# Gate pieces, head matrices, z accumulators and final states of one mLSTM and S5 step, placed anew

## The chip, the core and the metric

The kernel runs on one core of one Trainium2 chip. The metric is the device time of one execution in microseconds. Five engines work beside one another, each through its own instructions in order: TensorE (PE, matrix products and transposes), VectorE (DVE), ScalarE (ACT), GpSimd (POOL) and SyncE (SP), whose queue here issues nearly all DMAs.

## The reference, cut to what matters

One step of a layer with two head groups that share the input `a = rmsnorm(h)`, for a prompt of 1024 tokens and 32 sample tokens (8 sequences of 4):

```python
proj = a @ w_in
x_m, z_m, o_m, i_pre, f_pre, x_s, z_s = jnp.split(proj, SPLIT_IDX, axis=-1)
...
logf = jax.nn.log_sigmoid(f_pre.astype(f32) + b_fgate.astype(f32))
hA, C1, n1, m1 = mlstm_chunkwise(q, k, v, i_t, logf, C0.astype(f32), n0.astype(f32), m0.astype(f32))
...
yB, sre1, sim1 = s5_scan(x_s.astype(f32), sre0, sim0, lam_re, lam_im, log_dt,
                         B_re, B_im, C_re, C_im, s5_D)
yB = jax.nn.gelu(yB)
yB = yB * jax.nn.sigmoid(yB @ w_glu.astype(f32) + b_glu.astype(f32))
yB = yB * jax.nn.silu(z_s.astype(f32))
h = h + jnp.concatenate([hA, yB], axis=-1).astype(h.dtype) @ w_out
...
h = h + jax.nn.sigmoid(h @ w_ple_gate) * e
```

`mlstm_chunkwise` needs for each token and head a running maximum and a running sum of the gates `i` and `f` (the "gate arithmetic" below). `s5_scan` runs 32 channel groups with a 64-dim complex state each. The final states of both groups are outputs.

## The kernel before

Activations lie transposed in SBUF, split into a high and a low fp32 part (`aTh`, `aTl`), and each product of fp32 matrices is three matmuls (`mm3`, L118 to L121: high by high, low by high, high by low). The weights are split likewise: ScalarE casts the high part (`hi_*`, L112), and DVE or POOL subtracts it for the low part (`lo_*`, L113). The tokens are cut into three chunks of 256, 384 and 416 columns (`CH`).

In order of time the program has these stages: the input tiles, their norms and the first o-gate tile, to about 62 us; the projection x_s and the tables of the S5 part, to about 100 us; the S5 part, to about 266 us; the mLSTM heads, which begin with the projection x_m (`ps_xm`), to about 470 us; the output projection and the last gate to the end.

The S5 part works on eight units u0 to u7 of four channel groups. A unit (`s5_run`) loads its inputs `us`, multiplies them by a table `WV` into the accumulators `vr`, `vi`, rotates on DVE (`w`, L616 to L623), scans, rotates back (`v`, `xs_`), and multiplies by `tz` and `cs` into `py`; ScalarE and DVE then form the GELU (`sq`, `y`). Between these steps PE gets filler: the rest of the o gate (`o_rest`), four tiles of z_s and two of z_m. `take(cols)` draws matmuls from the filler until that many columns are issued; `FILL_A`, `FILL_B`, `FILL_C` are the amounts behind the three steps of a unit. A tile of z has three accumulators (`ps_zs`, `ps_zm`; two buffers); each is emptied by a tanh on ScalarE (L702) and a product on DVE that reads the accumulator again (L703), and the result `ztmp` goes to HBM.

`s5_final` ends the part: it forms the sample's last states (`sfr`, `sfi`), transposes them on PE (`tpf`), copies them on ScalarE into `ob`, of tag "w2" with one buffer, and sends them out; the prompt's state `fin` follows (`tpg`). Then the rest of the filler is drawn.

The instructions are put in order by a scheduler that goes by priorities and a cost estimate. Within `tc.manual_schedule` PE keeps the written order, and only instructions that are recorded outside of it (there the gate arithmetic and the head matrices) may be placed between. The gate arithmetic (L785 to L893) is recorded behind the S5 part: transposes `tpr` to rows, running sums and maxima in `rw`, `bb_`, `g_`, `M_`, a reshaping through a DMA (`er` from `ends`, L820 on), `mc`, `mp`, then `nM`, `nML`; transposes `tpk`; and the same for the sample (`tps`, `sr`, `srw`, `d_srow`, `senm`, `tpq`, `scol`). `smb` (L1296) reads `d_srow` later. The head matrices (L894 to L915) are `Gm`, four products of w_q and w_k from transposes `tpw` copied to `wT` and products `gps`, and `scT`, the transposed conv state (`tpv`).

Of the kernel before, what the change touches and what calls it, by code (L numbers as in the profile page):

```python
# [24 lines left out]
FILL_A, FILL_B, FILL_C = 15000, 2400, 4000  # L25
# [4 lines left out]
def tile_hymba(ctx: ExitStack, tc: tile.TileContext, d: dict, o: list):  # L30
# [636 lines left out]
    def s5_final():  # L667
# [23 lines left out]
        dma(o_pim[0, 0], ob[:, 64:128])  # L691

# [15 lines left out]
    def filler():  # L710
# [58 lines left out]
    SC = 128.0 ** -0.5
    colv = mlc.tile([128, 3, 32], F32, name="colv")  # L770
    scol = mlc.tile([96, 2, 4], F32, name="scol")
    senm = mlc.tile([128, 1], F32, name="senm")
    d_row = dram.tile([2, 4, 8, 128], F32, name="d_row")
    d_srow = dram.tile([3, 4, 32], F32, name="d_srow")
    cmask = mlc.tile([128, 128], F32, name="cmask")


    def gt_(shape, name):
        return gp_.tile(shape, F32, name=name)

    G.memset(cmask, 0.0)
    G.affine_select(out=cmask, in_=cmask, pattern=[[1, 128]], compare_op=ALU.is_ge, fill=NEG, base=0,
                    channel_multiplier=-1)

    fx = gates[:, 4:8, :]  # L785
    na, uu, zz, ww, pp = (gt_([128, 4, 9], n) for n in ("na", "uu", "zz", "ww", "pp"))
    V.scalar_tensor_tensor(na, fx, -1.0, fx, op0=MUL, op1=MIN)
    A.activation(uu, na, AF.Exp)
    V.tensor_scalar(zz, uu, 2.0, None, op0=ADD)
    V.reciprocal(zz, zz)  # L790
    V.tensor_tensor(zz, zz, uu, op=MUL)
    V.tensor_tensor(ww, zz, zz, op=MUL)
    V.tensor_scalar(pp, ww, 1.0 / 13, None, op0=MUL)
    for c_ in (11, 9, 7, 5, 3):
        V.scalar_tensor_tensor(pp, pp, 1.0 / c_, ww, op0=ADD, op1=MUL)
    V.scalar_tensor_tensor(pp, pp, 1.0, zz, op0=ADD, op1=MUL)
    lf = gt_([128, 4, 9], "lf")
    V.tensor_scalar(lf, fx, 0.0, None, op0=MIN)
    V.scalar_tensor_tensor(lf, pp, -2.0, lf, op0=MUL, op1=ADD)
    gin = gt_([128, 2, 4, 8], "gin")  # L800
    V.tensor_copy(gin[:, 0], gates[:, 0:4, 0:8])
    V.tensor_copy(gin[:, 1], lf[:, :, 0:8])

    rw = gp_.tile([32, 2, 128], F32, tag="rw", name="rw", bufs=1)
    tp = pg([32, 2, 128], "tpr")
    for i in range(2):
        T.transpose(tp[:, i, :], gin[:, i].rearrange("p h c -> p (h c)"), ident)
    V.tensor_copy(rw, tp)
    one1 = gt_([32, 1], "one1")
    V.memset(one1, 1.0)  # L810
    one = one1.to_broadcast([32, 128])
    bb_, g_, M_, m_ = (gt_([32, 128], n) for n in ("bb_", "g_", "M_", "m_"))
    V.tensor_tensor_scan(bb_, one, rw[:, 1, :], 0.0, op0=MUL, op1=ADD)
    V.tensor_tensor(g_, rw[:, 0, :], bb_, op=SUB)
    V.tensor_tensor_scan(M_, one, g_, -3.0e38, op0=MUL, op1=MAX)
    ends = gt_([32, 2], "ends")
    V.tensor_copy(ends[:, 0:1], M_[:, 127:128])
    V.tensor_copy(ends[:, 1:2], bb_[:, 127:128])
    er4 = gt_([4, 8, 2], "er4")
    dma(er4, ends)  # L820
    mc = gt_([4, 9], "mc")
    V.memset(mc[:, 0:1], 0.0)
    V.tensor_tensor_scan(mc[:, 1:9], er4[:, :, 0], er4[:, :, 1], 0.0, op0=MAX, op1=ADD)
    with tc.high_priority():
        dma(o_pm[0, 0].unsqueeze(1), mc[:, 8:9])
    mp = gt_([32, 1], "mp")
    dma(mp, mc[:, 0:8])
    V.tensor_scalar(M_, M_, mp, None, op0=MAX)
    V.tensor_tensor(m_, M_, bb_, op=ADD)
    nM = gp_.tile([32, 2, 128], F32, tag="rw", name="nM", bufs=1)  # L830
    V.tensor_scalar(nM[:, 0, :], M_, -1.0, None, op0=MUL)
    A.activation(nM[:, 1, :], M_, AF.Exp, scale=-1.0, bias=mp)
    with tc.high_priority():
        dma(d_row.rearrange("x h c t -> (h c) x t"), nM)
    nML = gt_([32, 1], "nML")
    V.tensor_copy(nML, nM[:, 0, 127:128])
    wl_, en_ = gt_([32, 128], "wl_"), gt_([32, 128], "en_")
    A.activation(wl_, g_, AF.Exp, bias=nML)
    A.activation(en_, m_, AF.Exp, scale=-1.0)
    tp = pg([128, 3, 32], "tpk")  # L840
    for i, t_ in enumerate((g_, wl_, en_)):
        T.transpose(tp[:, i, :], t_, ident[:32, :32])
    V.tensor_copy(colv[:, 0:3], tp)

    gs = gt_([32, 2, 4], "gs")
    V.tensor_copy(gs[:, 0], gates[:32, 0:4, 8])
    V.tensor_copy(gs[:, 1], lf[:32, :, 8])
    sr = gt_([4, 2, 32], "sr")
    tp = pg([4, 2, 32], "tps")
    for i in range(2):  # L850
        T.transpose(tp[:, i, :], gs[:, i, :], ident[:32, :32])
    V.tensor_copy(sr, tp)
    rs1, rs2 = gt_([4, 8, 4], "rs1"), gt_([4, 8, 4], "rs2")
    V.memset(rs1, 1.0)
    V.memset(rs1[:, :, 0:1], 0.0)
    V.memset(rs2, 0.0)
    V.memset(rs2[:, :, 0:1], NEG)
    m0 = gt_([4, 8], "m0")
    dma(m0, d["state_mlstm_m"][0].rearrange("b h -> h b"))
    sb, sg, sM, sm_ = (gt_([4, 8, 4], n) for n in ("sb", "sg", "sM", "sm_"))  # L860

    def fl(ap):
        return ap.rearrange("p b t -> p (b t)")

    V.tensor_tensor_scan(fl(sb), fl(rs1), sr[:, 1, :], 0.0, op0=MUL, op1=ADD)
    V.tensor_tensor(fl(sg), sr[:, 0, :], fl(sb), op=SUB)
    V.tensor_tensor_scan(fl(sM), fl(rs2), fl(sg), NEG, op0=ADD, op1=MAX)
    m0b = m0.unsqueeze(2).to_broadcast([4, 8, 4])
    V.tensor_tensor(sM, sM, m0b, op=MAX)
    V.tensor_tensor(sm_, sM, sb, op=ADD)  # L870
    smo = gt_([4, 8], "smo")
    V.tensor_copy(smo, sm_[:, :, 3])
    with tc.high_priority():
        dma(o_sm[0].rearrange("b h -> h b"), smo)
    srw = gt_([4, 3, 32], "srw")
    sx1, sx2, swl = gt_([4, 8, 4], "sx1"), gt_([4, 8, 4], "sx2"), gt_([4, 8, 4], "swl")
    V.tensor_scalar(srw[:, 0, :], fl(sM), -1.0, None, op0=MUL)
    V.tensor_tensor(sx1, m0b, sM, op=SUB)
    A.activation(srw[:, 1, :], fl(sx1), AF.Exp)
    A.activation(srw[:, 2, :], fl(sm_), AF.Exp, scale=-1.0)  # L880
    with tc.high_priority():
        dma(d_srow.rearrange("x h t -> h x t"), srw)
    V.tensor_tensor(sx2, sg, sM[:, :, 3:4].to_broadcast([4, 8, 4]), op=SUB)
    A.activation(swl, sx2, AF.Exp)
    tp = pg([32, 2, 4], "tpq")
    T.transpose(tp[:, 0, :], fl(sg), ident[:4, :4])
    T.transpose(tp[:, 1, :], fl(swl), ident[:4, :4])
    for i in range(3):
        V.tensor_copy(scol[32 * i:32 * i + 32, 0, :], tp[:, 0, :])
        V.tensor_scalar(scol[32 * i:32 * i + 32, 1, :], tp[:, 1, :], SC, None, op0=MUL)  # L890
    dma(senm, d_srow[2].rearrange("h t -> (h t)").unsqueeze(1))
    wq = mlc.tile([128, 4, 128], F32, name="wq")
    wk = mlc.tile([128, 4, 128], F32, name="wk")  # L893
# [664 lines left out]
```

## Time and profile before

| | us |
|---|---|
| median of 3 runs | 691.0 |
| lowest, highest run | 689.8, 698.46 |
| the profiled execution | 693.87 |
| its span | 692.2 |
| PE busy | 623.8 |
| DVE busy | 435.8 |
| ACT busy | 264.1 |

The span runs from the first to the last instruction of the profiled execution; the execution's time is 1.67 us longer. The profiled execution took 2.87 us more than the median. Busy times are sums over the instructions of an engine; matmuls overlap, so the time in which PE is busy is shorter than the sum of its instructions. The mean clock granted to PE was 0.958 of full speed.

### The profile page before, as it was taken

The numbers are of one execution on the slowest core, as the hardware profiler recorded it, in microseconds if no ns is written. First come the engines' busy times: TensorE is split into PE (matmuls) and PEld (weight loads), VectorE is DVE, ScalarE is ACT, GpSimd is POOL, SyncE is SP. The second block draws the span as 40 slices with busy tenths as digits, with TensorE's granted clock in tenths as the row PEclk, the third lists the DMA queues.
The fourth block names the chain that finished last, engine by engine and source line by source line (L and its number), as shares of the span: only waits on it lengthen the run. The fifth ranks groups of instructions, "written<-read, shape, count | busy, mean of one in ns | idle before, by whom it ended". The sixth has DMA issues, their size and how long they took to land.

```text
span 692.2 us, 11563 instructions
## 1 busy us (share of the span) xinstructions
PE 623.8 (90%) x4068; PEld 547.7 (79%) x4068; DVE 435.8 (63%) x1289; ACT 264.1 (38%) x643; POOL 163.5 (24%) x173
## 2 busy tenths in 40 slices
PE   3999998987998949999996898769999999999995
PEld 2898898976988949998995687636888876778885
DVE  4789788979898640578667898754222323656435
ACT  5555633323332314534345545344111424433232
POOL 5813000000000115224323655544110204001000
PEclk9999999989999979999998899969999999999999
DMA  8804435452444338200546637457631237313121
GB/s 276 234 24 97 118 87 163 116 122 57 107 114 113 94 80 236 61 1 32 159 129 176 198 91 229 142 175 214 206 118 65 92 132 259 107 52 131 41 83 61
DMA packets 109679, 86.34 MB, mean 125 GB/s; under 512 B 33263, under 2 KB 92547, under 8 KB 109622
## 3 DMA queue, kind: packets, MB, share of 16 engines
q1 hardware_dynamic: 109622, 85.61, 41.3%
q8 instruction: 32, 0.52, 0.4%
q14 instruction: 25, 0.20, 0.1%
HBM read 60.10 MB, written 25.49 MB: 124 GB/s over the span
## 4 chain that ended last, share of the span: by engine, by line
PE 62%; DVE 16%; DMA 9%; issue 4%; SPq 4%; ACT 3%; POOL 1%; POOLq 0%; DVEq 0%; ACTq 0%
PE po L1379 4%; PE po L1378 4%; PE po L1377 4%; SPq L36 4%; PE po L1486 4%; PE po L1487 3%; PE po L1488 3%; PE ps_xm L120 2%; PE ps_xm L121 2%; PE ps_xm L119 2%; PE ps_zm L120 2%; PE ps_zm L119 2%; PE ps_zm L121 2%; PE ps_o L119 2%; PE ps_o L120 2%
## 5 line engine op out<-in xcount | busy, mean ns | idle before, releaser
L1486 PE MATMUL po<-wgh,hTh 128*128 128x512 f32 (+1 forms) x136 | 52.1, 383 | 0.7 <-ACT g_t L1489 0.7
L1488 PE MATMUL po<-wgh,hTl 128*128 128x512 f32 (+1 forms) x136 | 51.5, 379 | 0.0
L1487 PE MATMUL po<-wgl,hTh 128*128 128x512 f32 (+1 forms) x136 | 51.4, 378 | 0.0
L119 PE MATMUL ps_o<-hi_o,aTh 128*128 128x264 f32 (+2 forms) x136 | 41.2, 303 | 1.5 <-DVE gates L235 0.8
L120 PE MATMUL ps_o<-lo_o,aTh 128*128 128x264 f32 (+2 forms) x136 | 39.8, 293 | 1.4 <-POOL lo_o L113 1.4
L121 PE MATMUL ps_o<-hi_o,aTl 128*128 128x264 f32 (+2 forms) x136 | 39.7, 292 | 0.0
L119 PE MATMUL ps_zs<-aTh,hi_zs 128*128 128x256 f32 (+2 forms) x96 | 34.0, 354 | 4.8 <-DVE ztmp L703 4.7
L119 PE MATMUL ps_xs<-aTh,hi_xs 128*128 128x256 f32 (+2 forms) x96 | 31.9, 332 | 3.1 <-DVE gates L235 1.7
L1377 PE MATMUL po<-woh,mh 128*128 128x512 f32 x80 | 33.3, 416 | 1.0 <-ACT mh L1364 1.0
L119 PE MATMUL ps_zm<-aTh,hi_zm 128*128 128x256 f32 (+2 forms) x96 | 32.9, 343 | 0.1
L121 PE MATMUL ps_zm<-aTh,lo_zm 128*128 128x256 f32 (+2 forms) x96 | 32.4, 338 | 0.0
L120 PE MATMUL ps_zm<-aTl,hi_zm 128*128 128x256 f32 (+2 forms) x96 | 32.3, 337 | 0.0
L1378 PE MATMUL po<-wol,mh 128*128 128x512 f32 x80 | 32.3, 404 | 0.0
L121 PE MATMUL ps_zs<-aTh,lo_zs 128*128 128x256 f32 (+2 forms) x96 | 32.3, 337 | 0.0
L1379 PE MATMUL po<-woh,mlo 128*128 128x512 f32 x80 | 32.3, 403 | 0.0
L120 PE MATMUL ps_zs<-aTl,hi_zs 128*128 128x256 f32 (+2 forms) x96 | 32.3, 336 | 0.0
L119 PE MATMUL ps_xm<-aTh,hi_xm 128*128 128x256 f32 (+2 forms) x96 | 31.9, 332 | 0.0
L121 PE MATMUL ps_xm<-aTh,lo_xm 128*128 128x256 f32 (+2 forms) x96 | 31.8, 332 | 0.0
L120 PE MATMUL ps_xm<-aTl,hi_xm 128*128 128x256 f32 (+2 forms) x96 | 31.6, 329 | 0.0
L121 PE MATMUL ps_xs<-aTh,lo_xs 128*128 128x256 f32 (+2 forms) x96 | 31.3, 326 | 0.0
L120 PE MATMUL ps_xs<-aTl,hi_xs 128*128 128x256 f32 (+2 forms) x96 | 31.0, 322 | 0.0
L1486 PEld LDWEIGHTS po<-wgh,hTh 128*128 128x128 f32 x136 | 25.6, 188 | 6.0 <-ACT g_t L1489 1.0
(591 smaller groups left out, 1931.7 us busy)
## 6 DMA issues: line engine op xcount, KB each, us to landing
xt<-in_x_prompt SPq DMA_DIRECT2D x15, 512.0 KB
Wraw<-in_w_out SPq DMA_DIRECT2D x16, 256.0 KB
Wraw<-in_w_ple_gate SPq DMA_DIRECT2D x16, 256.0 KB
d_h<-xt SPq DMA_DIRECT2D x8, 512.0 KB
h_t<-d_h SPq DMA_DIRECT2D x8, 512.0 KB
out<-g_t SPq DMA_DIRECT2D x14, 256.0 KB
mt<-d_m SPq DMA_DIRECT2D x10, 256.0 KB
d_us<-xs SPq DMA_DIRECT2D x32, 72.0 KB
```

The lines of the kernel that those rows point to most:

```text
L36: nc.sync.dma_start(out, in_)
L119: T.matmul(ps, wh, xh, start=first, stop=False)
L120: T.matmul(ps, wh, xl, start=False, stop=False)
L121: T.matmul(ps, wl, xh, start=False, stop=last)
L1377: T.matmul(ps, mh[:, k % 4, :], hi, start=k == 4, stop=False)
L1378: T.matmul(ps, mh[:, k % 4, :], lo, start=False, stop=False)
L1379: T.matmul(ps, mlo[:, k % 4, :], hi, start=False, stop=k == 3)
L1486: T.matmul(ps[:, :b - a], hTh[i][:, k, :], hi[:, ws], start=k == 4, stop=False)
L1487: T.matmul(ps[:, :b - a], hTh[i][:, k, :], lo[:, ws], start=False, stop=False)
L1488: T.matmul(ps[:, :b - a], hTl[i][:, k, :], hi[:, ws], start=False, stop=k == 3)
```

## The change

It does five things. The gate arithmetic becomes a generator `gates_g` in four pieces, and one piece is recorded at the end of each of the units u0 to u3, inside the block with the written PE order. The head matrices and their loads are recorded ahead of the S5 part. In the filler's z tiles ScalarE copies the accumulator to a tile `zc` in SBUF (one buffer), and DVE reads that. `s5_final` becomes a generator with filler between its pieces, and its second `ob` uses the tag "zr". The filler amounts grow. The bodies of the gate arithmetic and of the head matrices are unchanged; lines behind the S5 part get numbers 17 higher.

```diff
--- before.py
+++ after.py
-FILL_A, FILL_B, FILL_C = 15000, 2400, 4000
+FILL_A, FILL_B, FILL_C = 15500, 3600, 4400
...
             V.tensor_tensor(t_, t_, f1, op=ADD)
-        for t_, dst in ((sfr, o_sre), (sfi, o_sim)):
+        yield
+        for t_, dst, tag in ((sfr, o_sre, "w2"), (sfi, o_sim, "zr")):
             tp = pt([128, 128], "tpf")
             T.transpose(tp, t_.rearrange("p b q -> p (b q)"), ident)
-            ob = s5.tile([128, 128], F32, tag="w2", name="ob", bufs=1)
+            ob = s5.tile([128, 128], F32, tag=tag, name="ob", bufs=1)
             A.copy(ob, tp)
             dma(dst[0].rearrange("b (q g) p -> (b q) (g p)", g=2), ob)
+            yield
         tp = pt([32, 128], "tpg")
         T.transpose(tp, fin, ident)
         ob = s5.tile([32, 128], F32, tag="w3", name="ob2")
         A.copy(ob, tp)
         dma(o_pre[0, 0], ob[:, 0:64])
         dma(o_pim[0, 0], ob[:, 64:128])
+        yield
...
-    def z_tile_g(c0, idx, name):
+    def z_tile_g(c0, idx, name, free=None):
...
             A.activation(tz_[:, :n], ps[:, :n], AF.Tanh, scale=0.5)
+            if free is not None:
+
+                zc = free.tile([128, 416], F32, tag="zc", name="zc", bufs=1)
+                A.copy(zc[:, :n], ps[:, :n])
+                ps = zc
             V.scalar_tensor_tensor(tz_[:, :n], tz_[:, :n], 1.0, ps[:, :n], op0=ADD, op1=MUL)
...
+    def gates_g():
+
+        G.memset(cmask, 0.0)
...
+        rw = gp_.tile([32, 2, 128], F32, tag="rw", name="rw", bufs=1)
+        yield
+        tp = pg([32, 2, 128], "tpr")
...
+        A.activation(en_, m_, AF.Exp, scale=-1.0)
+        yield
+        tp = pg([128, 3, 32], "tpk")
...
+        A.activation(swl, sx2, AF.Exp)
+        yield
+        tp = pg([32, 2, 4], "tpq")
...
+        dma(senm, d_srow[2].rearrange("h t -> (h t)").unsqueeze(1))
+        yield
...
-            yield from z_tile_g(2056 + 128 * j, 4 + j, f"zs{j}")
+            yield from z_tile_g(2056 + 128 * j, 4 + j, f"zs{j}", s5)
         for h in range(2):
-            yield from z_tile_g(512 + 128 * h, h, f"zm{h}")
+            yield from z_tile_g(512 + 128 * h, h, f"zm{h}", s5)
...
+    for h in range(4):
+        tp = pg([128, 2, 128], "tpw")
...
+        A.mul(Gm[:, h, :], gps, SC)
     lo_engine[0] = V
     with tc.manual_schedule(engines={mybir.EngineType.PE}):
+        gate = gates_g()
         ins = [s5_in(u) for u in range(8)]
...
             take(FILL_C)
-        s5_final()
-        for _ in fill:
-            pass
+            if u < 4:
+                next(gate)
+        end = s5_final()
+        for n in (5000, 3000, 3000, 1 << 30):
+            prod(end)
+            take(n)
```

On PE at the end of S5, before (`ps_zm` is filler, `tpf` and `tpg` the transposes of final states):

```order
L119 MATMUL ps_zm_3071<-aTh_105,hi_zm_3008 128x384
L120 MATMUL ps_zm_3071<-aTl_108,hi_zm_3008 128x384
L121 MATMUL ps_zm_3071<-aTh_105,lo_zm_3009 128x384
L682 MATMUL tpf<-ident,sfr 128x128
L682 MATMUL tpf<-ident,sfi 128x128
L687 MATMUL tpg<-ident,fin 32x128
L119 MATMUL ps_zm_3071<-aTh_105,hi_zm_3008 128x384
```

The same place after the change:

```order
L121 MATMUL ps_zm_3287<-aTh_106,lo_zm_3212 128x416
L683 MATMUL tpf<-ident,sfr 128x128
L119 MATMUL ps_xm<-aTh_104,hi_xm_3419 128x256
...
L120 MATMUL ps_xm<-aTl_108,hi_xm_3419 128x384
L683 MATMUL tpf<-ident,sfi 128x128
L121 MATMUL ps_xm<-aTh_105,lo_xm_3420 128x384
...
L120 MATMUL ps_xm<-aTl_109,hi_xm_3419 128x416
L689 MATMUL tpg<-ident,fin 32x128
L121 MATMUL ps_xm<-aTh_106,lo_xm_3420 128x416
```

The three transposes stood together ahead of the rest of the z filler; now the filler has ended before the first, and matmuls of the first x_m tile lie between them.

On PE ahead of the products `vr` of u3, after the change (`tpW` makes the table `WV`, `tpk` and `tps` belong to the gates):

```order
L557 MATMUL tpW<-ident,wt 128x128 x4
...
L793 MATMUL tpk<-ident,g__2001 128x32
L793 MATMUL tpk<-ident,wl__2026 128x32
L793 MATMUL tpk<-ident,en__2027 128x32
L802 MATMUL tps<-ident,gs 4x32 x2
L612 MATMUL vr<-us,WV 64x144 x4
```

Before, these transposes lay among the filler of u0 and u1, wherever the scheduler had put them; `tpr` now stands in the same way ahead of the `vr` of u2, and `tpq` ahead of that of u4.

On DVE in u2, after the change (`er` comes by DMA from `ends`):

```order
L764 TENSOR_TENSOR g__2001<-rw,bb__2000 32x128
L768 COPY ends<-bb__2000 32x1
...
L767 COPY ends<-M__2002 32x1
L640 TENSOR_TENSOR xs__2061<-v_2064,v_2065 64x2x128 x2
L596 TENSOR_TENSOR rti<-rBr,rAi 128x256
L596 TENSOR_TENSOR rtr<-rBr,rAr 128x256
L641 TENSOR_TENSOR xs__2061<-v_2066,v_2067 64x2x128 x2
L773 SCALAR_TENSOR_TENSOR mc<-er_2010 4x8
```

Before, this arithmetic lay ahead of the first `w` of u0; now it lies between the rotations of u2, six instructions from the last `ends` to the scan `mc`.

## Rows read from the trace of the kernel before

**Rows 1.** The page's section 1: engine, busy us, share of the span, instructions.

```profile
PE 623.8 (90%) x4068; PEld 547.7 (79%) x4068; DVE 435.8 (63%) x1289; ACT 264.1 (38%) x643; POOL 163.5 (24%) x173
```

**Rows 2.** Windows, u0's approach and u0 to u7: stretch, elapsed, busy by engine, clock, DMA.

```profile
82.00:100.30 18.30, 18.30 (x119) 17.41 (x118) 12.46 (x33) 8.26 (x24) 0.11 (x1) 1.00 0.34 97
102.56:122.92 20.36, 18.22 (x212) 16.79 (x214) 16.97 (x44) 6.50 (x21) 0.11 (x1) 0.99 0.53 148
122.92:138.79 15.87, 15.87 (x133) 15.14 (x127) 15.14 (x48) 4.76 (x17) 0.10 (x1) 0.91 0.46 119
138.79:164.34 25.55, 21.00 (x150) 19.56 (x147) 20.03 (x56) 6.50 (x17) 0.11 (x1) 0.87 0.41 97
164.34:184.31 19.97, 16.37 (x107) 15.29 (x105) 16.74 (x42) 6.33 (x18) 0.11 (x1) 0.91 0.38 98
184.31:202.20 17.89, 16.84 (x130) 15.26 (x128) 16.84 (x43) 6.25 (x17) 0.11 (x1) 1.00 0.43 110
202.20:220.64 18.44, 16.38 (x109) 15.68 (x105) 15.07 (x40) 5.42 (x14) 0.10 (x1) 0.91 0.38 105
220.64:234.82 14.18, 14.18 (x108) 13.62 (x108) 9.08 (x29) 4.59 (x12) 2.56 (x1) 1.00 0.43 118
234.82:266.50 31.68, 22.50 (x129) 21.54 (x126) 15.11 (x45) 8.60 (x21) 7.09 (x4) 0.84 0.42 102
```

**Rows 3.** Waits of PE, 100 to 266.5 us: total, times, longest, all us.

```profile
PE tpg L687 <- ACT ob L684: 8.7, 1, 8.7
PE ps_zs L119 <- DVE ztmp L703: 4.7, 2, 2.7
```

**Rows 4.** Timeline of PE, 247 to 260 us: start, length, line, tiles, idle before.

```profile
247.90 0.34 PE L121 MATMUL ps_zm<-aTh,lo_zm 128*128 128x384 f32 x1
...
257.74 0.39 PE L687 MATMUL tpg<-ident,fin 128*32 128x128 f32 x1 [8.71 <-ACT ob L684]
...
259.85 0.52 PE L119 MATMUL ps_zm<-aTh,hi_zm 128*128 128x384 f32 x1
```

**Rows 5.** Timeline of ScalarE (ACT), 241 to 263 us.

```profile
241.85 0.51 ACT L702 ACTIVATE ztmp<-ps_zm 128x416 f32<-128x416 f32 x1
...
257.42 0.27 ACT L684 COPY ob<-tpf 128x128 f32<-128x128 f32 x1 [8.77 <-DMA out<-ob]
...
262.04 2.00 ACT L928 CAST hi_g<-raw_g 128x1024 fp32r<-128x1024 f32 x2 [3.61 <-DMA out<-ob]
```

**Rows 6.** Timeline of SP's DMA issues, 247 to 263 us.

```profile
255.60 2.46 SPq L36 DMA_DIRECT2D out<-ob  x2
```

**Rows 7.** Groups by line, PE, 140 to 200 us: busy, mean ns, idle before.

```profile
L909 PE MATMUL tpw<-ident,wq 128*128 128x128 f32 x4 | 1.2, 299 | 0.8 <-ACT Gm L915 0.8
```

**Rows 8.** Groups by line, DVE, 60 to 160 us: first and last of eleven.

```profile
L808 DVE COPY rw<-tpr 32x256 f32<-32x256 f32 x1 | 0.4, 405 | 0.0
...
L836 DVE COPY nML<-nM 32x1 f32<-32x1 f32 x1 | 0.1, 133 | 0.0
```

**Rows 9.** Waits of DVE, 80 to 266.5 us.

```profile
DVE xs L272 <- DMA er<-ends: 5.4, 1, 5.4
DVE smb L1296 <- DMA smb<-d_srow: 5.3, 1, 5.3
```

**Rows 10.** Timeline of SP's DMA issues, 82 to 92 us.

```profile
87.51 0.73 SPq L36 DMA_DIRECT2D er<-ends  x1
...
90.07 0.29 SPq L36 DMA_DIRECT2D out<-mc  x1
```

**Rows 11.** Groups by line, DVE, 100 to 266.5 us.

```profile
L616 DVE TENSOR_TENSOR w<-vr,rtr 128x256 f32<-128x256 f32 x8 | 3.3, 416 | 2.7 <-PE vr L612 2.7
...
L635 DVE TENSOR_TENSOR v<-zi,rti 128x256 f32<-128x256 f32 x8 | 3.3, 415 | 0.0
```

**Rows 12.** Timeline of DVE, 244 to 247 us.

```profile
245.24 0.58 DVE L703 SCALAR_TENSOR_TENSOR ztmp<-ztmp,ps_zm 128x416 f32<-128x416 f32 x1
```

More of the change, by code (lines that the diff above doesn't have):

```diff
@@ L732, in tile_hymba @@
             s5_x(j, c)
+    wq = mlc.tile([128, 4, 128], F32, name="wq")
+    wk = mlc.tile([128, 4, 128], F32, name="wk")
+    wv = mlc.tile([128, 4, 128], F32, name="wv")
+    for t_, nm in ((wq, "w_q"), (wk, "w_k"), (wv, "w_v")):
+        dma(t_, d[nm][0].rearrange("h p e -> p h e"))
+    Gm = mlc.tile([128, 4, 128], F32, name="Gm")
+    scT = mlc.tile([128, 4, 24], F32, name="scT")
+    scr = gt_([24, 512], "scr")
+    dma(scr, d["state_conv"][0].rearrange("b j e -> (b j) e"))
+    tp = pg([128, 4, 24], "tpv")
+    for h in range(4):
+        T.transpose(tp[:, h, :], scr[:, 128 * h:128 * h + 128], ident[:24, :24])
+    V.tensor_copy(scT, tp)
+    for h in range(4):
+        tp = pg([128, 2, 128], "tpw")
+        T.transpose(tp[:, 0, :], wq[:, h, :], ident)
+        T.transpose(tp[:, 1, :], wk[:, h, :], ident)
+        wT = pw.tile([128, 2, 128], F32, tag="wT", name="wT", bufs=1)
+        A.copy(wT, tp)
+        gps = pg([128, 128], "gps")
+        T.matmul(gps, wT[:, 0, :], wT[:, 1, :], start=True, stop=True)
+        A.mul(Gm[:, h, :], gps, SC)
     lo_engine[0] = V
     with tc.manual_schedule(engines={mybir.EngineType.PE}):
+        gate = gates_g()
         ins = [s5_in(u) for u in range(8)]
@@ L761, in tile_hymba @@
             take(FILL_C)
-        s5_final()
-        for _ in fill:
-            pass
+            if u < 4:
[4 more added lines that the diff above has]
+            take(n)
     lo_engine[0] = G
     s5x.close()
[L769 to L893, printed above, removed]
@@ L894, in tile_hymba @@
-    wv = mlc.tile([128, 4, 128], F32, name="wv")
-    for t_, nm in ((wq, "w_q"), (wk, "w_k"), (wv, "w_v")):
-        dma(t_, d[nm][0].rearrange("h p e -> p h e"))
-    Gm = mlc.tile([128, 4, 128], F32, name="Gm")
-    scT = mlc.tile([128, 4, 24], F32, name="scT")
-    scr = gt_([24, 512], "scr")
-    dma(scr, d["state_conv"][0].rearrange("b j e -> (b j) e"))
-    tp = pg([128, 4, 24], "tpv")
-    for h in range(4):
-        T.transpose(tp[:, h, :], scr[:, 128 * h:128 * h + 128], ident[:24, :24])
@@ L905, in tile_hymba @@
-    V.tensor_copy(scT, tp)
-    for h in range(4):
-        tp = pg([128, 2, 128], "tpw")
-        T.transpose(tp[:, 0, :], wq[:, h, :], ident)
-        T.transpose(tp[:, 1, :], wk[:, h, :], ident)
-        wT = pw.tile([128, 2, 128], F32, tag="wT", name="wT", bufs=1)
-        A.copy(wT, tp)
-        gps = pg([128, 128], "gps")
-        T.matmul(gps, wT[:, 0, :], wT[:, 1, :], start=True, stop=True)
-        A.mul(Gm[:, h, :], gps, SC)
     CG = ((0, 288), (256, 256), (512, 256), (768, 256))
```

107 lines of the change are left out of this document (added).

## The prediction, as it was put down before the changed kernel ran

> **What bounds the kernel now.** I began with the busy shares [rows 1]. PE, the matmul engine, is busy 90% of the span, so only what gives PE time back matters: 692.2 - 623.8 = 68 us in which it does nothing, and what it spends at the lower clock. DVE at 63% counts only where PE waits for it.
>
> Next came windows cut at the first `w` product of each S5 unit on DVE, u0 to u7 in order [rows 2]. A unit is one turn of the loop that the change edits, so the elapsed column is its pitch. Compare elapsed, PE busy and DVE busy in each row: u1 and u6 have PE full (15.87 of 15.87, 14.18 of 14.18), while u2 takes 25.55 and u7 with what follows 31.68, and in those neither engine is full. The eight sum to 163.9 us, PE's busy time in them to 141.4. The first row of the group is 82 to 100 us, ahead of u0: PE is full, 18.30 of 18.30.
>
> Then the waits of PE in that stretch [rows 3]: 8.7 us in one wait of `tpg` for ScalarE's copy `ob`, and 4.7 in two waits of `ps_zs` for DVE's `ztmp`.
>
> The 8.7 us has a visible cause. `tpg` starts at 257.74 after 8.71 us of idle PE [rows 4]. ScalarE's second `ob` copy waited 8.77 us for the DMA out of the first [rows 5], since both use one buffer, and SP came to issue that DMA only at 255.60 [rows 6], behind the S5 results. After the pause PE ran slowly: a matmul of 128x384 at 259.85 lasts 0.52 us where one of the same shape and tile took 0.34 at 247.90 [rows 4]; the clock granted over that unit is 0.84 [rows 2]. A pause costs its length and a slow stretch behind it.
>
> **The change part by part.**
>
> *Head matrices ahead of S5.* Eight `tpw`, eight `gps` and four `tpv` leave the S5 part. A `tpw` takes 0.30 us [rows 7], pipelined to about half that, so the twenty take some 3 us of PE. They now lie among the o-gate matmuls of the first stage, where PE has work too, so up to 3 us is paid there. Against that, DVE loses ahead of u0 the eleven rows of gate arithmetic from `rw` to `nML`, 2.8 us [rows 8], and its 5.4 us wait for `er` [rows 9]. As 82 to 100 us is PE's, this relief buys little. For the start of u0 I take no shift, with -3 and +3 as ends. The loads of the matrices stay among the same neighbours on SP's queue.
>
> *Gates in pieces.* Four pieces, behind u0 to u3. The transposes `tpr`, `tpk`, `tps`, `tpq` get fixed places ahead of `vr`; the eleven DVE rows go into u2, the sample's gate rows into u3. Two DMA round trips come along, `ends` to `er` and `srw` to `smb`. For both DVE waited in the trace, 5.4 and 5.3 us [rows 9]. In the new order the scan that reads `er` stands six DVE instructions behind the last copy to `ends`, some 2.5 us at 0.4 each [rows 11]; `smb` stands 17 behind `srw`. SP issued `er` at 87.51, and at 90.07 the result of the scan that reads it [rows 10]: 2.6 us is the round trip with the scan when SP is free. Each wait lies between 0 and 5.4; I take 1.2 in u2 and as much in u3, nearest to the case in which SP is not late.
>
> *Accumulators emptied by ScalarE.* Each z chunk gets one more ScalarE copy, 18 in all. The nearest row is the tanh of such a chunk, 0.51 us [rows 5], so 9 us of ScalarE over eight units, in each of which it is busy 4.6 to 8.6 us [rows 2]: hidden. The accumulator is then freed by ScalarE, not DVE. That takes away the 4.7 us of `ps_zs` waits [rows 3] and the slow stretches behind them.
> DVE's own instruction keeps its price: a product that reads PSUM (L616) takes 416 ns, one of the same size from SBUF (L635) 415 ns [rows 11]. The Trainium skill, "Perfetto Trace Analysis", section "Optimizing Scalar/DVE Operations", gives an overhead of about 60 ns for DVE on SBUF and 125 ns on PSUM; by that an estimate would be 18 x 65 ns = 1.2 us less of DVE. The trace does not show this difference.
>
> *Final states spread, two buffers.* The second `ob` has a buffer of its own, and filler lies between the pieces. The 8.7 us wait goes, and with it a slow stretch of about 2 us (12 matmuls of 384 columns, each 0.18 longer).
>
> *Filler sizes.* 21,400 columns a unit become 23,500, so that the filler ends with u7. This moves PE work between units and costs nothing by itself.
>
> **The sum by unit.** A unit takes the longer of PE's and DVE's work, plus the waits left. PE: 141.4, less about 10 of slow clock (the clock column's shortfall times elapsed is 13.6, part of it idle), less the 3 moved, is 128, or 16.1 a unit. DVE: its busy time [rows 2], plus or minus what moved.
> u0 20.4 to 19.9: its first waits, for a weight load, stay. u1 15.9 to 17.1: one more low-part cast on DVE. u2 25.6 to 20.5: DVE 20.0 less 1.6 (the cast and `scol` out, the eleven rows in) is 18.4; the `smb` wait leaves, 1.2 for `er` and 0.9 of small gaps come. u3 20.0 to 20.2: 16.7 and 2.3 of gates are 19.0, and 1.2 of waits. u4 17.9 to 17.0: DVE was busy 16.84, and its pause for the head matrices goes. u5 18.4 to 16.2: PE's floor. u6 14.2 to 16.2: more filler is left for it. u7 31.7 to 17.0: DVE 15.1, PE 16.1, and gaps.
> Sum 144.1 against 163.9: **-19.8 us**.
>
> *Given back later.* ScalarE's cast `hi_g` waited 3.61 us for memory that S5 held [rows 5], while PE stood still anyway. With that pause gone, `hi_g` and the `xm` evacuation behind it come nearer to the path. Ends 0 and +5 (that wait and some slow clock); I take +2.
>
> Total -19.8 + 0 + 2 = -17.8. The profiled execution took 693.87 us (span 692.2 and 1.67 around it), so 676.1 in such an execution; it stood 2.9 above the median of 691.0. **Predicted median: 673 us.** This case's own range, by the ends above, is 665 to 680.
>
> **The rivals.**
> A. *DMA waits move into the units at full price.* DVE runs in order: a late `er` or `mp` holds the `sq` and `w` behind it, then `vr`, then PE, which restarts slowly. For it: both waits did happen [rows 9], and SP now has `raw_zm`, `tz` and a `d_z` ahead of `er`. Against: the distances above. Price: two waits of 5.3 for the 2.4 taken, 8.2, and about 2 of slow clock: 673 + 10 = 683. Chance 0.23.
> B. *The pause was needed.* `hi_g` is late behind S5's memory and PE waits at the head of the mLSTM stage, 7 us and more instead of 2: 679. For it: its row [rows 5]. Against: only one wait of that kind is seen. Chance 0.08.
> C. *The single `zc` buffer makes it slower.* ScalarE runs in order too: the copy to `zc` waits until DVE has read the one before, with `WV`, `sq` and `ks` behind it. In the trace DVE's part of a chunk ran at 245.24 [rows 12], 2.9 us after its tanh (241.85 and 0.51 long [rows 5]). If half of the 18 copies wait that long on the loop's path: 18 x 2.9 / 2 = 26 us, so -18 + 26 = +8: 699 us, slower than before. It decides once an evacuation costs over 1 us on the path, 18 us in all. Against: a z tile's three accumulators take PE some 11 us, so DVE has three or four for each, and ScalarE is idle more than half of every unit. Chance 0.05. The Trainium skill, "VectorE: DVE Perf Modes", section "Rules for kernel authors", speaks for C: accept reading the matmul output from PSUM, or copy it to SBUF first if many operations follow. Here one follows; rows 3 show PE waiting for the accumulator, which the rule does not weigh.
> D. *It does more.* PE is full from u4 and DVE meets no wait in u0 to u3: -28 instead of -18, 663. Chance 0.09.
> The change not doing what it says is hardly a case for `ob`: the tile has another tag. The main case has 0.55.
>
> **Numbers.** 2% of 691 is 13.8 us, about what a measurement can tell from no change here: faster is below 677.2, slower above 704.8. Faster: 0.85 of the main case, D, and a little of A and B, 0.60. Same: the rest of those and most of C, 0.37. Slower: C's far end, 0.03. The range for 8 in 10 is 662 to 688, from D to A with somewhat longer waits.
>
> **What would show it.** `tpg` waits less than 1 us, and no 9 us gap of PE lies near the last unit. `ps_zs` does not wait for `ztmp`; if it waits for `zc`, C is under way. Pitches near 20 in u2 and u3 and 16 to 17 after; 25 in u2 or u3 with DVE waiting for a DMA is A. PE waits just behind the start of `xm` are B. I am wrong if u0's `w` comes later than 106 us (it came at 102.56), or if PE waits for `gates` or head matrices in the first stage.

## The result, and the profile after

Over 18 executions of each kernel the changed one takes 688.83 us (684.59 to 692.64), the kernel before 693.29 (689.8 to 698.46): a ratio of 0.9929, 95% interval 0.9905 to 0.9952. That is faster by 4.5 us, where 18 were forecast and the range ended at 688; by the prediction's border of 2% it counts as the same, which had a chance of 0.37. The execution that was profiled took 686.29 us (span 684.6), 2.5 us less than the median, so the two profiled executions differ by 7.6 us and not by 4.5.

The windows from `w` to `w`, u0 to u7 in order, answer to [rows 2]; the columns are stretch, elapsed, busy time of PE, PEld, DVE, ACT and POOL, granted clock, DMA share and GB/s:

```profile
100.81:122.47 21.66, 20.21 (x226) 18.75 (x222) 16.82 (x42) 6.47 (x21) 0.11 (x1) 1.00 0.49 138
122.47:139.64 17.17, 17.16 (x160) 16.16 (x159) 16.93 (x42) 5.82 (x16) 0.11 (x1) 1.00 0.52 124
139.64:161.96 22.32, 16.28 (x103) 15.50 (x104) 18.78 (x56) 6.12 (x18) 0.10 (x1) 0.89 0.43 111
161.96:184.77 22.81, 20.73 (x155) 18.91 (x152) 18.57 (x57) 6.87 (x21) 0.11 (x1) 0.95 0.31 85
184.77:202.74 17.97, 13.97 (x85) 13.23 (x85) 16.82 (x42) 6.06 (x17) 0.11 (x1) 0.91 0.44 112
202.74:219.45 16.71, 15.81 (x120) 14.87 (x118) 15.01 (x38) 6.27 (x17) 0.11 (x1) 1.00 0.44 115
219.45:235.75 16.30, 15.82 (x120) 14.90 (x118) 11.93 (x29) 6.26 (x16) 2.61 (x1) 1.00 0.41 109
235.75:251.70 15.95, 15.28 (x102) 14.84 (x99) 13.89 (x36) 5.45 (x14) 2.48 (x1) 1.00 0.23 66
```

They sum to 150.9 us against 163.9 before, and u0's `w` comes at 100.81 instead of 102.56, so `x_m` starts at 251.7 instead of 266.5: 14.8 us earlier, of 19.8 forecast. u7 takes 15.95 us, where the sum had 17.0 and the kernel before 31.68. The reader should look at u2 and u3, 22.32 and 22.81, where 20.5 and 20.2 were expected. The waits of DVE there (total, times, longest) answer to [rows 9]. The one for `er` lies in u2, the one for `smb` in u3:

```profile
DVE smb L1313 <- DMA smb<-d_srow: 3.8, 1, 3.8
...
DVE mc L773 <- DMA er<-ends: 2.2, 1, 2.2
```

SP's timeline shows how they come about (start, length, issue):

```profile
146.65 0.62 SPq L36 DMA_DIRECT2D tz<-dK  x1
147.36 0.46 SPq L36 DMA_DIRECT2D d_z<-ztmp  x1
147.92 0.73 SPq L36 DMA_DIRECT2D er<-ends  x1
151.76 0.30 SPq L36 DMA_DIRECT2D out<-mc  x1
...
167.86 0.25 SPq L36 DMA_DIRECT2D d_srow<-srw  x1
...
173.12 0.33 SPq L36 DMA_DIRECT2D senm<-d_srow  x1
173.49 0.42 SPq L36 DMA_DIRECT2D smb<-d_srow  x1
```

`smb` reads what `d_srow` wrote, so its issue stood 5.6 us behind that of `d_srow`, and DVE came to `smb` 3.8 us before it had landed. The last copy to `ends` ended at 146.88 on DVE; SP was then at `tz` and a `d_z`, and issued `er` one microsecond later. From that issue to the issue of the result (`out` from `mc`) it was 3.8 us, where [rows 10] had 2.6. PE has a wait that no row of before had; the second row is all that is left of [rows 3]:

```profile
PE tps L802 <- DVE colv L794: 3.4, 1, 3.4
...
PE ps_zs L119 <- ACT zc L709: 0.9, 1, 0.9
```

`tps` needs the one accumulator that `tpk` uses, and that comes free when DVE copies `colv`, which stands behind arithmetic for the tables of the next unit on DVE. This wait lies at the end of u2, ahead of the `vr` of u3. In total PE waited longest for DVE's `xs` ahead of `py`, 8.4 us in six waits of 0.5 to 3.1 us, against one of 1.8 before. The kernel without the gate pieces (no_gates, below) has 9.0 us of these, so the pieces are not their cause. The 8.71 us of [rows 4] have gone. `tpf` for sfi and `tpg` run between `x_m` matmuls and wait for nothing:

```profile
255.55 0.27 PE L683 MATMUL tpf<-ident,sfi 128*128 128x128 f32 x1
...
259.37 0.27 PE L689 MATMUL tpg<-ident,fin 128*32 128x128 f32 x1
```

What S5 gained is not what the kernel gained. From the first `x_m` matmul to the end, before:

```profile
266.50:692.20 425.70, 396.18 (x2415) 332.72 (x2413) 234.09 (x630) 161.26 (x386) 119.28 (x116) 0.96 0.40 126
```

and in the changed kernel:

```profile
251.70:684.60 432.90, 402.98 (x2417) 336.16 (x2415) 237.22 (x638) 163.96 (x396) 127.81 (x118) 0.95 0.41 128
```

The number of matmuls is the same but for the two last transposes, the sum of idle PE time too (425.70 - 396.18 = 29.5 us, 432.90 - 402.98 = 29.9), but PE is busy 6.8 us longer: the same work at a lower clock on average. Half of the 14.8 us was given back behind S5. By the median executions it is more: the median less 1.67 us and the start of `x_m` leaves 425.1 us before and 435.5 after. Below, this figure is called **the later stages by the median**. It takes the start of `x_m` in one trace for that of all executions, so a few microseconds of it are uncertain. The expectations below have 424 for it before.

### The profile page after: what moved, and what is told of

It reads as the page before. It is cut to its first block, busy times and chain, and to the rows that moved or that the text cites. A ratio compares the mean times of both kernels' runs of the same rounds, so it can differ in the third digit from the quotient of the medians.

```text
span 684.6 us, 11565 instructions
## 1 busy us (share of the span) xinstructions
PE 625.3 (91%) x4068; PEld 547.0 (80%) x4068; DVE 441.8 (65%) x1289; ACT 268.4 (39%) x661; POOL 166.7 (24%) x173
## 4 chain that ended last, share of the span: by engine, by line
PE 58%; DVE 15%; DMA 14%; issue 4%; ACT 3%; POOL 3%; SPq 2%; POOLq 0%; DVEq 0%; ACTq 0%
PE po L1396 4%; PE po L1395 4%; PE po L1394 4%; PE po L1505 3%; PE po L1503 3%; PE po L1504 3%; PE ps_o L119 2%; PE ps_o L120 2%; PE ps_o L121 2%; SPq L36 2%; DMA Wraw<-in_w_ple_gate 2%; DMA Wraw<-in_w_out 2%; PE ps_xs L119 2%; PE ps_xs L120 2%; PE ps_zm L119 1%
## 5 line engine op out<-in xcount | busy, mean ns | idle before, releaser
L1397 DVE TENSOR_TENSOR xt<-xt,po 128x512 f32<-128x512 f32 x16 | 11.0, 687 | 57.1 <-PE po L1396 53.5
L1396 PE MATMUL po<-woh,mlo 128*128 128x512 f32 x80 | 33.7, 421 | 0.0
```

The source lines that it names most:

```text
L1396: T.matmul(ps, mlo[:, k % 4, :], hi, start=False, stop=k == 3)
L1397: V.tensor_tensor(xt[:, cs], xt[:, cs], ps, op=ADD)
```

## The experiments

All ratios are against the kernel before, run beside on the same chip.

### One part at a time

Each of these is the kernel before with one part of the change, at the old filler amounts; the amounts, the fifth part, were not tried alone. The expectations name two theories of what was given back behind S5: A, that the later stages take longer whenever they start earlier, whatever their order, and B, that their new order costs it.

```diff
 # spread_only: the generator s5_final, second ob in "zr", filler between
 # gates_only:  gates_g, with next(gate) behind u0 to u3
 # heads_only:  wq to Gm recorded ahead of S5
 # zc_only:
-            yield from z_tile_g(2056 + 128 * j, 4 + j, f"zs{j}")
+            yield from z_tile_g(2056 + 128 * j, 4 + j, f"zs{j}", s5)
```

spread_only. 

> The kernel before with only the last part of the change: second ob in its own buffer, filler between the pieces of s5_final. Both theories: the 8.7 us wait of tpg and the slow stretch behind it go, x_m starts near 256 instead of 266.5 us. Theory A (the mLSTM and output stages lived on that pause and give time back whatever their order is): they take about 5 us longer, total 5 to 6 us below before. Theory B (only the new order of the later stages costs): their order is nearly that of before, so 9 to 11 us below before.

gates_only. 

> The kernel before with only the gate arithmetic in four pieces at u0 to u3. The later stages keep their order. Theory A1 (the pieces bring DVE's waits for DMA, 2 to 4 us each, and PE's wait for the gate accumulator into u2 and u3): u2 and u3 together 45 us as in the changed kernel, DVE waiting for er and smb there, total within 2 us of before. Rival A2 (these waits come from the other parts): u2 and u3 together under 42 us, total 3 to 5 us below before.

heads_only. 

> The kernel before with only the head matrices ahead of S5. First w of u0 moves by -1 to +3 us, the waits for wT and Gm (1.8 us) go and some 3 us of PE work leaves the units; x_m starts 1 to 3 us earlier. Later stages keep their order. Theory A: 0 to 1 us of it left in the total; theory B: 1 to 3 us.

zc_only. 

> The kernel before with only the copy of the z accumulators by ScalarE. The 4.7 us of ps_zs waits for ztmp go and two slow stretches with them: x_m starts 4 to 6 us earlier. Theory A: half of it left, total 2 to 3 us below before. Theory B: 4 to 6 us below, unless its later stages, which the scheduler orders anew, take longer.

| kernel | median, us | ratio (95%) | x_m starts, us | later stages, profile / by the median |
|---|---|---|---|---|
| before | 693.04 | | 266.5 | 425.7 / 424.9 |
| spread_only | 683.08 | 0.9865 (0.9835 to 0.9894) | 253.5 | 427.9 / 427.9 |
| zc_only | 684.66 | 0.9894 (0.9862 to 0.9925) | 257.5 | 423.5 / 425.5 |
| heads_only | 689.25 | 0.9937 (0.9914 to 0.9961) | 262.0 | 426.0 / 425.6 |
| gates_only | 696.32 | 1.0044 (1.0018 to 1.007) | 267.7 | 427.3 / 427.0 |

Three parts bring 10.0, 8.4 and 3.8 us, one costs 3.3; the sum is -18.9 us, close to the -17.8 of the prediction, though the parts together gave 4.5. Their shifts of `x_m` add up to 25 us. spread_only came out as theory B had it (9 to 11 us). zc_only and heads_only gained more than either theory had, since `x_m` came 9.0 and 4.5 us earlier, where 4 to 6 and 1 to 3 were expected. In spread_only the last unit is filled as the prediction had it, PE 19.46 of 19.58 us:

```profile
233.92:253.50 19.58, 19.46 (x126) 18.89 (x123) 14.20 (x37) 5.27 (x14) 2.52 (x1) 1.00 0.29 74
```

In zc_only no `ps_zs` wait is left among PE's waits of 0.3 us and more; these two are the largest, the first of them the one that spread_only removes:

```profile
PE tpg L689 <- ACT ob L685: 8.7, 1, 8.7
PE vr L612 <- ACT WV L559: 6.2, 2, 4.4
```

In gates_only the units u2 and u3 are 47.6 us together, above the 45 of theory A1 and the 45.5 of the kernel before; the total, which A1 had within 2 us of before, is 3.3 us longer:

```profile
137.79:161.02 23.23, 16.76 (x109) 15.89 (x110) 19.65 (x57) 6.81 (x17) 0.10 (x1) 0.87 0.43 109
161.02:185.42 24.40, 21.41 (x133) 19.59 (x130) 17.76 (x53) 6.08 (x18) 0.10 (x1) 0.77 0.32 82
```

with the same two waits of DVE (`smb` shorter than A1 had it),

```profile
DVE mc L773 <- DMA er<-ends: 2.9, 1, 2.9
...
DVE smb L1313 <- DMA smb<-d_srow: 1.2, 1, 1.2
```

and PE waiting 2.5 us for the transposes `tpk` at their fixed place, beside the old wait for `ob`:

```profile
PE tpg L689 <- ACT ob L685: 9.7, 1, 9.7
...
PE tpk L793 <- ACT wl__1966 L788: 2.5, 1, 2.5
```

### The changed kernel with one part taken back or moved

Here theory A says that the waits found for the part in question hold S5 up, so that `x_m` moves when the part is taken back or moved, and rival O that the other parts fill the same gaps.

```diff
 # no_gates: gates_g recorded in one go behind S5, as before
-            if u < 4:
-                next(gate)
+    for _ in gates_g():
+        pass
 # no_zc: z accumulators read by DVE from PSUM
 # pool_smb:
-    V.tensor_tensor(smb, smb, smask, op=ADD)
+    G.tensor_tensor(smb, smb, smask, op=ADD)
 # spaced: pool_smb, and yields in gates_g behind dma(er4, ends), behind dma(mp, ...), ahead of gs
-            if u < 4:
+            if u < 7:
                 next(gate)
```

no_gates. 

> The changed kernel with the gate arithmetic recorded in one go behind S5 as before, all else as changed; the later stages keep the order they have in the changed kernel. Theory A (the gate pieces are the step that fails: their waits are what u2 and u3 still have): u2 and u3 together 38 to 40 us instead of 45, x_m starts near 245 us instead of 252, total 5 to 8 us below the changed kernel. Rival O (the other parts fill the same gaps, so little is left however the gates lie): x_m starts at 250 or later, total within 2 us of the changed kernel. For the later stages: if they take longer the earlier they start, over 436 us to the end and most of the lead is lost; if it is their order that costs, 433 us as in the changed kernel.

no_zc. 

> The changed kernel with the z accumulators read by DVE from PSUM as before. Alone the copy brought 8 us. Theory A: its waits for the accumulator come back in full beside the gate pieces, x_m starts 5 to 8 us later than in the changed kernel, total 5 to 8 us more. Rival O: the gaps are shared, within 3 us of the changed kernel.

pool_smb. 

> The changed kernel with the two additions into smb on GpSimd instead of DVE, so that the 3.8 us wait for the DMA smb no longer stands in DVE's order. Theory A (that wait holds DVE, then vr, then PE): u3 19 us instead of 22.8, x_m starts 3 to 4 us earlier, total 2 to 4 us below the changed kernel. Rival (DVE's later wait for something else takes its place, or PE had slack): u3 stays at 22 us and the total within 1 us.

spaced. 

> The changed kernel with the gate arithmetic in seven pieces over u0 to u6 and the smb additions on GpSimd: tpk ahead of vr of u5, tps of u6, tpq of u7. PE's 3.4 us wait of tps for colv goes, and the smb wait with it; the wait for er stays in u2. Theory A: u2 and u3 together 38 to 40 us, x_m starts 5 to 7 us earlier than in the changed kernel, total 4 to 6 us below it. Rival O: u5 to u7 grow by what u2 and u3 lose, total within 2 us.

| kernel | median, us | ratio (95%) | u2, u3, us | x_m starts | later stages, profile / by the median |
|---|---|---|---|---|---|
| changed | 688.83 | 0.9929 (0.9905 to 0.9952) | 22.3, 22.8 | 251.7 | 432.9 / 435.5 |
| no_gates | 681.67 | 0.9861 (0.9816 to 0.9906) | 17.9, 19.2 | 244.4 | 438.9 / 435.6 |
| no_zc | 686.62 | 0.9935 (0.9907 to 0.9963) | 22.2, 22.9 | 257.2 | 430.9 / 427.8 |
| pool_smb | 680.94 | 0.9853 (0.9809 to 0.9897) | 22.7, 19.0 | 249.0 | 433.3 / 430.3 |
| spaced | 673.5 | 0.974 (0.9698 to 0.9782) | 21.3, 16.8 | 246.7 | 426.0 / 425.1 |

For S5, theory A holds four times. With the gates in one go u2 and u3 lose 8 us, and `x_m` starts 7.3 us earlier, though DVE still has all of that arithmetic to do:

```profile
141.52:159.43 17.91, 14.64 (x111) 13.63 (x110) 15.60 (x48) 5.16 (x15) 0.11 (x1) 1.00 0.50 125
159.43:178.60 19.17, 16.01 (x105) 15.47 (x105) 18.07 (x45) 6.19 (x17) 0.11 (x1) 0.91 0.45 114
```

With `smb` off DVE u3 loses 3.8 us, as much as that wait was, and `x_m` starts 2.7 us earlier:

```profile
163.02:182.03 19.01, 18.31 (x138) 16.58 (x135) 18.16 (x55) 6.78 (x21) 0.89 (x3) 0.95 0.40 104
```

Spread wider, in spaced, `tps` no longer waits for `colv`, u2 and u3 take 38.1 us together and `x_m` starts 5.0 us earlier. Without the copy `zc`, `x_m` starts 5.5 us later.

The totals do not follow. no_zc, expected 5 to 8 us slower than the changed kernel, lost 5.5 us in S5 and is no slower; its later stages are 8 us shorter by the median (2 in the profiles). pool_smb and spaced are 7.9 and 15.3 us faster than the changed kernel, where 2 to 4 and 4 to 6 were expected; what goes beyond their gain in S5 lies behind it. no_gates has PE's rows of the later stages in the very order of the changed kernel, starts them 7.3 us earlier and takes as long by the median (its profiled execution took 3.5 us more than its median, and 438.9 there). Two more sets of kernels agree: heads_only and gates_only have the order of the kernel before, but for one pair of rows in gates_only, and by the median all three take 424.9 to 427.0 us. So an earlier start alone costs little or nothing. That speaks for their order.

### Is it the order of the later stages?

Behind S5 the scheduler places the instructions by its own estimate of time, so a change in S5 can give it another order there. The expectations name theory R, that this order sets the length of the later stages, and rival S, that the order does not matter and something else does, such as the earlier start. First came a second trace and three kernels that change something else as well:

```diff
 # svm_dve (the changed kernel) and spaced_svm (spaced):
-            G.tensor_tensor(vm[:, :nb], v3.bitcast(F32).unsqueeze(1).to_broadcast([96, nb, 129]),
+            V.tensor_tensor(vm[:, :nb], v3.bitcast(F32).unsqueeze(1).to_broadcast([96, nb, 129]),
 # spread_zc: the kernel before with spread_only and zc_only together
```

after_again. 

> The changed kernel once more, for a second trace. If its order of the later stages makes them long, they take 432 to 437 us from the start of x_m again, with PE idle and slow clock there near 51 us together; if the first trace was a chance, 425 to 428.

svm_dve. 

> The changed kernel with the product svm of the sample heads on DVE instead of GpSimd, where it stands behind an addition that waits for a DMA. S5 stays as in the changed kernel, x_m near 252 us. Theory R (the new order of the later stages puts short waits of PE where the clock is lost with each): PE's 3.4 us of waits of sups for svm go, and the later stages take 425 to 430 us instead of 433 to 435; total 5 to 8 us below the changed kernel. Rival S (they take longer because they start earlier): 433 us or more, total within 2 us of it.

spaced_svm. 

> The seven pieces and the smb additions on GpSimd, and svm on DVE. x_m starts near 247 us as with the seven pieces alone. Theory R: sups no longer waits for svm (3.9 us there), total 2 to 4 us below the 673.5 of the seven pieces, if the order that the scheduler finds does not bring other waits; rival S: no gain.

spread_zc. 

> The kernel before with two parts of the change, the final states spread and the z accumulators copied, old filler sizes, gates and head matrices as before. Alone they brought 10.0 and 8.4 us. If gaps are not shared (theory A) x_m starts near 245 us, 13 and 9 us earlier than before, and the total is 18 us below before or a few us more where the later stages are ordered badly; if shared (rival O) x_m starts after 250 us and the total is 11 to 13 us below.

The second trace gave 688.43 us, `x_m` at 252.5 and 434.2 us behind it, so the length of the later stages was not a chance of one execution. svm_dve took 696.82 us (1.0053, 1.0027 to 1.0079), 439.1 us behind `x_m` in its profile, and spaced_svm 685.59 (0.9911, 0.988 to 0.9942), 438.0: both theories of svm missed. `sups` waited for svm 4.6 and 3.8 us on DVE, 3.4 and 3.9 on GpSimd, and the order changed too, so they tell nothing apart. spread_zc started `x_m` at 243.5 us, so the two gains do add up in S5 (23.0 for 13.0 and 9.0), but took 680.58 us (0.9829, 0.9789 to 0.9869), 435.4 behind it by the median: 12.2 us below before, where 18 were expected.

Then came changes of the filler amounts alone, by 100 or 200 columns (in ng_oldfill back to the old amounts). They are meant to change little but the scheduler's order:

```diff
-FILL_A, FILL_B, FILL_C = 15500, 3600, 4400
+FILL_A, FILL_B, FILL_C = 15600, 3600, 4400   # fill_15600
+FILL_A, FILL_B, FILL_C = 15500, 3500, 4400   # fill_3500
+FILL_A, FILL_B, FILL_C = 15000, 2400, 4000   # ng_oldfill (from no_gates)
+FILL_A, FILL_B, FILL_C = 15100, 2400, 4000   # before_fill (from the kernel before)
+FILL_A, FILL_B, FILL_C = 15500, 3400, 4400   # fill_3400, ng_3400 (from no_gates)
```

fill_15600. 

> The changed kernel with 100 columns more filler in the first step of a unit (FILL_A 15600). x_m starts within 1.5 us of the changed kernel's 252 us; the order of the later stages differs (6% of PE's rows there). Theory R (the order sets their length): it differs from the changed kernel's 434 to 436 us by several us, either way, and the total with it. Rival S (the kernel's other properties set it): 434 to 436 us, total within 2 us of the changed kernel.

fill_3500. 

> The changed kernel with 100 columns less filler in the second step (FILL_B 3500); 20% of PE's rows in the later stages stand elsewhere. x_m within 1.5 us of 252. Theory R: later stages away from 434 to 436 us by 3 us or more, more likely shorter, total with them. Rival S: total within 2 us of the changed kernel.

before_fill. 

> The kernel before with 100 columns more filler in the first step (FILL_A 15100), its later stages in another order (5% of PE's rows). x_m within 2 us of 266.5. Theory R: later stages differ from 424 us by several us, more likely longer, total 692 to 702. Rival S: 424 us, total within 2 us of before.

ng_oldfill. 

> The changed kernel with the gate arithmetic in one go as before and the old filler sizes. x_m starts at 244 to 246 us as with the gates in one go alone; the later stages are ordered otherwise (34% of PE's rows). Theory R: they take 424 to 440 us, not bound to the 435 of the kernel with the gates in one go; total 670 to 686. Rival S: 435 us, total 680 to 682.

By theory R each new order of the later stages has a length of its own, and 435 was an unlucky one. These four did not do that. fill_15600 took 688.45 us and fill_3500 692.35, 434.2 and 437.6 us behind `x_m` by the median, ng_oldfill 682.06 and 436.9; before_fill took 689.28, 423.7, with `x_m` at 263.9. So a new order does not by itself change the length: in these the later stages stay near 435 where the kernel comes from the changed one and near 424 where it comes from the kernel before. Most of the long kernels share one thing in PE's rows: the products `snps` of the last of the four sample heads end behind the last `ps_g`, the products of the GLU (`w_glu`). In the kernel before it is the other way round (shortest, median and longest, first and last start):

```profile
L1186 PE MATMUL snps<-sc,sqm x64: 273/273/298, 317.2 to 433.6; 128*32 128x129 f32 x64
```

```profile
L119 PE MATMUL ps_g<-yh,hi_g x64: 276/282/609, 377.1 to 435.8; 128*128 128x256 f32 x48, 128*128 128x288 f32 x16
```

In the changed kernel:

```profile
L1203 PE MATMUL snps<-sc,sqm x64: 273/273/298, 306.3 to 426.9; 128*32 128x129 f32 x64
```

```profile
L119 PE MATMUL ps_g<-yh,hi_g x64: 276/282/587, 367.2 to 422.5; 128*128 128x256 f32 x48, 128*128 128x288 f32 x16
```

With 200 columns less in FILL_B (not 100) the scheduler gives another order. Matched by accumulator and shape in the traces, some 93% of PE's rows of the later stages stand in it as in the kernel before, and 62% as in the changed kernel. That made a test in which R had to name the number.

fill_3400. 

> The changed kernel with FILL_B 3400 instead of 3600, nothing else. x_m starts near 252 us as in the changed kernel. The later stages have nearly the order of the kernel before, the last sample head early among the GLU matmuls. Theory R (the order costs the 10 us): they take 424 to 428 us, total 678 to 682. Rival S (the earlier start costs, whatever the order): 433 to 437 us, total 687 to 691.

ng_3400. 

> The changed kernel with the gates in one go as before and FILL_B 3400. x_m starts near 244.5 us, the later stages in the same order as in fill_3400. Theory R: 424 to 428 us, total 670 to 674, below every kernel so far. Rival S: 435 us or more, total 680 to 684.

| kernel | median, us | ratio (95%) | x_m starts | later stages, profile / by the median |
|---|---|---|---|---|
| fill_3400 | 681.04 | 0.9837 (0.9808 to 0.9866) | 253.9 | 425.1 / 425.5 |
| ng_3400 | 672.42 | 0.9701 (0.9674 to 0.9729) | 243.7 | 428.3 / 427.1 |

Both came out as R had them. In fill_3400 `x_m` starts 2.2 us later than in the changed kernel, and the kernel is 7.8 us faster (6.4 by the two ratios):

```profile
253.90:679.00 425.10, 398.53 (x2417) 335.58 (x2415) 237.18 (x638) 163.58 (x395) 128.24 (x118) 0.96 0.41 131
```

The last `snps` now lies ahead of the last `ps_g`, among the GLU's matmuls:

```profile
L1203 PE MATMUL snps<-sc,sqm x64: 273/273/298, 305.1 to 414.2; 128*32 128x129 f32 x64
```

```profile
L119 PE MATMUL ps_g<-yh,hi_g x64: 276/285/683, 364.4 to 417.1; 128*128 128x256 f32 x48, 128*128 128x288 f32 x16
```

ng_3400 has the same order, but for one pair of rows, 10.2 us earlier, and keeps all but 1.6 us of it. It is the fastest of all the kernels, 3.0% below before:

```profile
243.70:672.00 428.30, 396.15 (x2416) 331.52 (x2414) 238.42 (x638) 164.28 (x395) 127.08 (x118) 0.97 0.41 130
```

So kernels with one and the same PE order have later stages within about 2 us of each other by the median: 434.3 to 435.6 (the changed kernel, its second trace, no_gates), 424.9 to 427.0 (before, heads_only, gates_only), 425.5 and 427.1 (these two). But likeness of order is no rule. Measured in the same way, ng_oldfill has 92% of these rows as in the kernel before and takes 436.9 us, and spaced has 89% as in the changed kernel and takes 425.1. So either a small piece of the order matters, or something besides PE's order does, and that R named the right number for fill_3400 by its likeness to before was partly luck.

## Why the prediction was wrong

**What held.** The views named the right waits. The 8.7 us of `tpg` and the waits for accumulators went, alone worth 10.0 and 8.4 us in the total, and spread_zc shows that their gains in S5 add up. u1, u5, u6 and u7 came within 1.1 us of their numbers (17.17, 16.71, 16.30, 15.95), and u0's `w` came 1.75 us earlier, within the ends given. ScalarE's copies were nearly hidden: what rival C feared, ScalarE waiting for the single `zc` buffer, did come,

```profile
ACT zc L709 <- DVE ztmp L711: 7.4, 4, 2.6
```

but PE waited only 0.9 us for it, and zc_only gained 8.4 us. The rule of the Trainium skill behind C ("VectorE: DVE Perf Modes", section "Rules for kernel authors") advises the copy only where many operations follow. Here one follows, and the copy paid, because it frees an accumulator for which PE waited. DVE's product did not become cheaper by it: 416 columns took 554 to 591 ns from SBUF after the change and 576 to 589 from PSUM before. The Trainium skill, "Perfetto Trace Analysis", section "Optimizing Scalar/DVE Operations", gives overheads from which 65 ns a piece less would be an estimate; the traces do not show it.

**The step that failed first: "Gates in pieces".** The sum took 1.2 us of waits in u2 and as much in u3. Measured were 2.2 for `er`, 3.8 for `smb`, and 3.4 of PE for `tps`, which the sum had not at all. I had priced both nearest to the case in which SP is not late, with the 2.6 us of [rows 10] as the round trip; `er` took 3.8 from its issue and was issued 1 us late, and the issue of `smb` alone stood 5.6 us behind the write it reads. The two DMA waits are the mechanism of rival A, 6.0 us where A had 10.6; the wait of `tps` for the accumulator stood in no rival. pool_smb shows `smb` (u3 from 22.8 to 19.0), spaced removes `tps` too, and no_gates the whole: `x_m` 7.3 us earlier. Alone the part costs 3.3 us in the total. u0 and u4 added 1.8 and 1.0 us to the miss.

**The step that failed worse: "Given back later".** It had +2 us with an end of +5, for `hi_g` and S5's memory. Measured were 7.2 us in the profiled pair and about 10 by the medians, and not for that reason: in the first 40 us from the start of `x_m` the longest wait of PE is

```profile
PE vps L1055 <- ACT xm L1023: 0.3, 1, 0.3
```

The order that the scheduler plans for everything behind S5 had changed too (matched as above, some 62% of PE's rows there stand as before), and the part of the order that I compared ended at S5: a new order was put at nothing without a reason. fill_3400, with 200 columns of filler less and another order, is 7.8 us faster. With the gate step taken out as well, ng_3400 stands 19.9 us below the kernel before in its own round (672.42 against 692.32), where 17.8 were forecast, and its later stages take 2.6 us more than those of before in the profiles, near the +2 of the sum. So the two steps together account for the size of the miss. The other terms held in their total but not one by one: alone the copy moved `x_m` by 9.0 us and the head matrices by 4.5, where the sum had 4.7 us of waits with their slow stretches for the one and 3 us of PE's work for the other.

**What stays open.** Which piece of the order costs the 10 us. The last sample head behind the GLU goes with the long kind in most kernels, but ng_oldfill and spread_zc have 435 to 437 us with it ahead of or near the GLU's end, and the shorter zc_only, no_zc and spaced have it 1.1 us behind, so it is a mark rather than a shown cause. No experiment moved that head alone, and none changed the later order with S5 left exactly as it was.

## What to carry to other kernels

Where a scheduler orders the program, a change in one stage is a change in all stages behind it: compare the order to the end of the program, and test a result with a small change of some amount that should not matter before believing or rejecting the edit. A DMA round trip moved into a loop brings its whole length with it and what stands ahead of it on the queue, and a transpose at a fixed place brings the wait for its accumulator: price both from the row of the same wait, not from the distance in the order. Parts that were timed one by one (here -10.0, -8.4, -3.8 and +3.3 us) show in one round which of them to leave out.

## What was not expected of the hardware

PE's time behind S5 is about 381 us of work in the kernels compared here, once idle time and the shortfall of the clock (the time by one less the granted clock, summed over the records of the later stages) are taken off. Before it is 425.7 less 29.5 idle and 15.2 of clock, 381.0; after, 432.9 less 29.9 and 21.3, 381.7; in no_gates 380.7, in spaced 382.1. Over all 20 traces it lies between 377.6 and 386.4. So kernels differ there in how long PE is idle (26.6 to 35.1 us) and in how long it runs at half clock.

The sum of PE's waits hardly differs between before and after, 22.1 us each by the list of waits. What differs is the shortfall of the clock, and that difference lies in one stretch, 160 to 230 us behind the start of `x_m`, where the last heads and the start of the output projection stand. Before:

```profile
426.50:496.50 70.00, 58.65 (x400) 43.25 (x399) 40.11 (x126) 28.30 (x57) 32.59 (x31) 0.88 0.63 196
```

After:

```profile
411.70:481.70 70.00, 57.02 (x370) 41.99 (x371) 36.35 (x129) 25.89 (x55) 30.90 (x29) 0.80 0.60 184
```

These figures of the clock are means over pieces at full and at half clock: 8.4 us of shortfall before, 14.0 after. The waits were spread otherwise, and went with more slow time; what in their spread does it was not tried. fill_3400 gains on the changed kernel by both: 26.6 us idle, and 18.0 of shortfall over its later stages.
